# Given SBUF places modulo 256 in every stage, and Newton's root in the first feed-forward of a decoder trunk

## The chip, the core and the metric

The kernel runs on one core of a Trainium2 chip. The metric is the device time of one execution in microseconds (us), as a median of runs. Five engines work side by side: TensorE (PE in the profile; its weight loads are listed apart as PEld), VectorE (DVE), ScalarE (ACT), GpSimd (POOL) and SyncE (SP), which issues most DMAs. Their operands lie in SBUF, 128 partitions wide; TensorE's results land in PSUM.

## The reference

Two layers work on 512 tokens of 1024 features, all in float32. Each layer is a half-step feed-forward, a mixer (a convolution module in layer 0, native sparse attention in layer 1), a second half-step feed-forward, and a gated input embedding; a norm closes the whole.

```python
def rms_norm(x, g):
    xf = x.astype(jnp.float32)
    y = xf * lax.rsqrt(jnp.mean(xf * xf, axis=-1, keepdims=True) + RMS_EPS)
    return (y * g.astype(jnp.float32)).astype(x.dtype)

def swiglu(x, wg, wu, wd):
    return (jax.nn.silu(x @ wg) * (x @ wu)) @ wd
...
    for i in range(DEPTH):
        x = x + 0.5 * swiglu(rms_norm(x, ffn1_norm[i]), ffn1_w_gate[i], ffn1_w_up[i], ffn1_w_down[i])
        h = rms_norm(x, mix_norm[i])
        ...  # conformer_conv for i = 0, nsa_mixer for i = 1
        x = x + 0.5 * swiglu(rms_norm(x, ffn2_norm[i]), ffn2_w_gate[i], ffn2_w_up[i], ffn2_w_down[i])
        gate = jax.nn.sigmoid(rms_norm(x, ple_norm[i]) @ ple_w_gate[i])
        x = x + gate * (p[i] @ ple_w_in[i])
    return rms_norm(x, final_norm)
```

The feed-forward is 1024 -> 2816 -> 1024, twice per layer.

## The kernel before, in words

**Layout.** Activations are held transposed: eight tiles of 128 features x 512 tokens. A matmul has a 128x128 block of a weight as its stationary operand (loaded by LDWEIGHTS) and an activation tile of 512 or 256 tokens as its moving operand.

**Three matmuls for one.** Both operands are split into a high part that the fast float32r format holds exactly and the rest: a weight into `wh` and `wl` (ScalarE copies the high part, line 292; VectorE subtracts, line 294), an activation into two tiles likewise. `mm3` (lines 353 to 358) issues high x high (L356), high weight x low activation (L357), low weight x high activation (L358). Nearly all of TensorE's time in the profile stands under these three lines, so the names of the tiles tell the stages apart: `out<-moving,stationary`.

**Feed-forward.** `ffn` (line 543) goes through 22 tiles of 128 hidden features. The first two are plain: 8 input tiles, 512 columns, moving tiles `s`. The others go in pairs (`pairs`, line 495): a 2x2 block product over two hidden tiles and two halves of 256 tokens with seven products instead of eight, from sums and differences of blocks. Its moving tiles are halves of `s` (the input itself) and `px` (differences of input blocks, made once per feed-forward by `right_sums`, line 475); its stationary tiles are `wh`/`wl` (weights and their combinations, made by `combine`) and `s1hl` (a sum of weights, split, made by `first_sums`, line 320). In one pair, with gate and up taken together, TensorE issues 48 matmuls on `s`, 24 on `px`, 24 on `px` against `s1hl`, 24 on `px`, then twice 12 on `s` and 12 on `px`, all of 256 columns. The gated result is split into `hid` tiles, which are the moving operands of the down projection, 512 columns.

**The norm.** The input is scaled by the gain alone, and the token's factor is multiplied in afterwards. Squares are added up in `acc` (line 432). `token_sums` (line 445) sums `acc` over features by four tiny matmuls against a column of means, `v` adds epsilon (L467), `rsqrt` (line 436) raises it to -0.5 on POOL (L438), and `spread` (L451, L458) turns the result into a tile `R` by four transposes. In the very first feed-forward the input comes straight from DMA, and `acc` is finished while TensorE is already at work on the plain tiles; `SUMS_AT = 3` places the sums in the second plain tile's gate product.

**Order.** The engines run their queues in order. A scheduler at build time orders the instructions from the code's order, priorities (`high_priority`) and explicit ties (`issue_after`): an instruction so tied is placed in the order behind the one it names. Weight splits run a few units ahead of their use (`ahead`, line 334). `behind` ties the splits of pair weights to the last `px` (`righted`).

**Places.** SBUF is given out by pools: constants, weights (`raw`, `wh`, `wl`), slots (`s`, 24 of them), tiny tiles, and a pool per stage (`phase`), whose tags are laid down in the order in which they are first asked for. So where a tile lies, modulo 256 bytes, follows from the sizes ahead of it.

Of the kernel before, what the change touches and what calls it, by code (L numbers as in the profile page):

```python
# [21 lines left out]
TAPS = 31  # L22
X_W1, WARM = 4, 18
OUTS = 2
CONV_FIN = 0
# [10 lines left out]
SUMS_AT = 3  # L36
# [159 lines left out]
class Kern:  # L196
    def __init__(self, ctx, tc, aps):
        self.ctx, self.tc, self.nc = ctx, tc, tc.nc
        self.a = aps
        pool = lambda name, **kw: ctx.enter_context(tc.tile_pool(name=name, **kw))  # L200
        self.cpool = pool("consts", bufs=1)
        self.wpool = pool("weights", bufs=1)
        self.spool = pool("slots", bufs=1)
        self.tiny = pool("tiny", bufs=2)
        self.ppool = pool("ps", bufs=1, space=PSUM)
        self.dpool = pool("dram", bufs=1, space=DRAM)
        self.uid = 0
        self.raw, self.hl, self.sums = {}, {}, {}
        self.unskewed = []
        self.HLB, self.held, self.now = 5, set(), None  # L210
        self.next_raw = self.next_split = 0
# [9 lines left out]

    def ptile(self, tag, n, w=512, dt=F32):
        self.uid += 1
        return self.phase.tile([128, w], dt, name=f"{tag}{self.uid}", tag=tag, bufs=n)
# [44 lines left out]
    def _split(self, what, j):  # L269
# [26 lines left out]
        if pair:  # L296
            with self.behind():
                self.first_sums(j)
# [5 lines left out]
    def combine(self, what, j):  # L304
# [4 lines left out]
        lo, hi = slice(0, HU // 2), slice(HU // 2, HU)  # L309
        q = self.sums[j]  # L310
        if what == "c":
            nc.vector.tensor_tensor(q[:, lo], u[:, lo], t[:, lo], op=OP.subtract)
            nc.vector.tensor_tensor(u[:, lo], t[:, hi], q[:, lo], op=OP.subtract)
# [4 lines left out]
        self.hl[what, j] = (h, l)  # L318

    def first_sums(self, j):  # L320
# [7 lines left out]
        nc.vector.tensor_tensor(u[:, lo], u[:, lo], u[:, hi], op=OP.add)  # L328
        hl = self.ptile("s1hl", 2, HU, F32R)
# [4 lines left out]
    def ahead(self, e):  # L334
# [3 lines left out]
        self.loads()  # L338
        while self.next_split < e:
# [100 lines left out]

    def token_sums(self, p, tiles):
# [19 lines left out]
    def rfin(self, acc):  # L461

        with self.tc.high_priority(FIN_PRI):
# [4 lines left out]
            r = self.rsqrt(v, 4)  # L468
# [74 lines left out]
    def ffn(self, n, i, nxt):  # L543
# [4 lines left out]
        fin = self.rfin(self.acc)  # L548
# [5 lines left out]
        for pi, fs in enumerate(PARTS):  # L554
# [9 lines left out]
            if pi == 0:  # L564
                assert PLAIN == 2
                first = (n, i) == (1, 0)
# [23 lines left out]
                if first:  # L590
                    with self.tc.issue_after(self.squared), self.tc.issue_after(self.vins):
                        for k in range(KD // 2):
                            self.right_sums(f"ffn{n}_norm", i, k)
                else:
# [3 lines left out]
                for f, pg, pu in wait:  # L598
                    gr = self.tmp()
                    nc.vector.tensor_tensor(pg, pg, R, op=OP.mult)  # L600
                    nc.scalar.activation(gr, pg, AF.Silu)
                    gated(f, gr, pu)
            for f in fs[::2]:
# [3 lines left out]
                G = next(both)  # L607
# [104 lines left out]
    def glu(self, c, pa, pg, ta=None):  # L712
# [4 lines left out]
        with self.tc.high_priority(FIN_PRI):  # L717
            nc.vector.tensor_tensor(pg, pg, self.R, op=OP.mult)
            nc.scalar.activation(pg, pg, AF.Sigmoid, bias=self.col("conv_b_pw1", KD + c))
            if CONV_ON[c] == "pe":  # L720
                u = self.ptile("uu", 2, PH * (SP + LAGS - 1)).rearrange("p (q s) -> p q s", q=PH)
# [4 lines left out]
            else:  # L726
                u = self.ptile("u", 3, S + TAPS - 1)
# [103 lines left out]
    def conv(self, nxt):  # L831
# [3 lines left out]
        self.dwc = self.phase.tile([128, KD, TAPS], F32, name="dwc")  # L835
# [159 lines left out]
    def put_k(self, g):  # L995
        nc, t, KT = self.nc, self.kt, self.KTs[g % 2]
        for br, sl, ot in ((0, slice(0, 64), slice(64, 128)), (1, slice(64, 128), slice(0, 64))):
            nc.scalar.activation(KT[sl, 0, br, 32:], t[sl], AF.Copy)
            nc.vector.tensor_tensor(KT[sl, 1, br, 32:], t[sl], KT[sl, 0, br, 32:].bitcast(F32), op=OP.subtract)
            nc.sync.dma_start(KT[ot, :, br, 32:].bitcast(F32), KT[sl, :, br, 32:].bitcast(F32))  # L1000
# [74 lines left out]
    def cmp_in(self, j, first):  # L1075
# [15 lines left out]
        for gp, p in wait:  # L1091
            for s in range(2):
                t = self.ptile("e", EB, 516)
# [54 lines left out]
    def scores(self, job):  # L1148
# [16 lines left out]
        for a in range(HPG):  # L1165
            Q = self.Q[g, a // 2][:, a % 2, qt * 128:qt * 128 + 128]
            src, e = {}, self.slot() if a == HPG - 1 else self.ptile("e", EB, 516)
# [109 lines left out]
    def osplit(self, g):  # L1277
        nc = self.nc
        for pr in range(2):
            t = self.OT[g][pr]  # L1280
            h, l = (self.slot(F32R) if g < 2 else self.ptile("e", EB, 516, F32R)[:, :512] for _ in range(2))
# [26 lines left out]
    def nsa(self, nxt):  # L1308
# [3 lines left out]
        P = self.phase  # L1312
# [3 lines left out]
        self.pos = P.tile([128, 2, 16], F32, name="pos")  # L1316
        nc.gpsimd.dma_start(self.pos, self.a["pos"])
        self.rowmask = P.tile([128, 1], F32, name="rowmask")
        nc.gpsimd.dma_start(self.rowmask, self.a["rowmask"])
        self.gates = P.tile([128, 4, 48], F32, name="gates")  # L1320
        self.gates0 = P.tile([128, 16], F32, name="gates0")
        self.kc = P.tile([128, G, 32], F32, name="kc")
        self.ec = P.tile([128, 4, HPG, 32], F32, name="ec")
# [4 lines left out]
        self.ects = [P.tile([128, 2, 512], F32R, name=f"ect{i}") for i in range(2)]  # L1328
# [111 lines left out]
    def run(self):  # L1440
        def phase():
            return self.tc.tile_pool(name="phase", bufs=1, reuse_waits="tile")
# [3 lines left out]
        for i in range(L):  # L1446
            self.tb = 4
# [84 lines left out]
```

## Time and profile before

| what | value |
|---|---|
| runs | 2019.25 us median of 3 (2018.37 to 2019.88) |
| profiled execution | 2018.77 us, its span 2016.7 us |
| TensorE busy | 1992.7 us, 99% of the span |
| VectorE busy | 1546.0 us, 77% |
| ScalarE / POOL busy | 1100.5 us, 330.7 us |
| matmuls recorded | 12534 |

In a row of a group stand the line of the kernel, the engine, the operation, `out<-in` by the program's names without buffer numbers (`b` is a bank of PSUM), partitions x elements, the count, then the busy time in us and the mean duration of one in ns, and behind the second bar the engine's idle time ahead of these instructions and who ended it. A timeline row begins with the start and the duration in us. A matmul's recorded duration is longer than the distance to the next one's start, since matmuls overlap in the pipeline.

### The profile page before, as it was taken

The numbers are of one execution on the slowest core, as the hardware profiler recorded it, in microseconds if no ns is written. First come the engines' busy times: TensorE is split into PE (matmuls) and PEld (weight loads), VectorE is DVE, ScalarE is ACT, GpSimd is POOL, SyncE is SP. The second block draws the span as 40 slices with busy tenths as digits, with TensorE's granted clock in tenths as the row PEclk, the third lists the DMA queues.
The fourth block names the chain that finished last, engine by engine and source line by source line (L and its number), as shares of the span: only waits on it lengthen the run. The fifth ranks groups of instructions, "written<-read, shape, count | busy, mean of one in ns | idle before, by whom it ended". The sixth has DMA issues, their size and how long they took to land.

```text
span 2016.7 us, 32709 instructions
## 1 busy us (share of the span) xinstructions
PE 1992.7 (99%) x12534; PEld 1789.7 (89%) x12534; DVE 1546.0 (77%) x2703; ACT 1100.5 (55%) x1972; POOL 330.7 (16%) x365
## 2 busy tenths in 40 slices
PE   8999999999999999999999999999999999999998
PEld 7989999888789898988999989888888789998987
DVE  8869777795687796777968868646889797786875
ACT  7535445662665363555644535437888665363543
POOL 0000000352300000012000000557666200000022
PEclk9999999999999999999999999999999999999999
DMA  4323323466425244243232322463333023232241
GB/s 170 105 96 104 126 74 105 180 206 202 141 97 166 86 144 136 97 133 118 84 115 95 115 87 90 162 182 116 95 90 104 25 99 120 95 116 94 94 141 59
DMA packets 79483, 235.16 MB, mean 117 GB/s; under 512 B 8848, under 2 KB 16160, under 8 KB 79328
## 3 DMA queue, kind: packets, MB, share of 16 engines
q1 hardware_dynamic: 78368, 230.69, 34.6%
q8 instruction: 98, 1.61, 0.3%
q0 software_dynamic: 816, 2.33, 0.3%
q14 instruction: 57, 0.47, 0.1%
q10 hardware_dynamic: 144, 0.07, 0.0%
HBM read 214.66 MB, written 16.29 MB: 115 GB/s over the span
## 4 chain that ended last, share of the span: by engine, by line
PE 91%; DVE 6%; ACT 2%; issue 1%; DMA 0%; SPq 0%; POOL 0%; DVEq 0%; POOLq 0%; ACTq 0%
PE b L356 28%; PE b L357 27%; PE b L358 27%; PE b L821 2%; PE b L1180 1%; PE b L1244 1%; PE b L1263 1%; PE b L1119 1%; PE b L1264 1%; DVE s L415 1%; DVE t L482 1%; DVE wl L294 1%; DVE px L491 0%; DVE acc L432 0%; DMA raw<-in_w 0%
## 5 line engine op out<-in xcount | busy, mean ns | idle before, releaser
L356 PE MATMUL b<-s,wh 128*128 128x256 f32 (+1 forms) x1408 | 448.8, 320 | 0.6 <-ACT wh L292 0.5
L357 PE MATMUL b<-s,wh 128*128 128x256 f32 (+1 forms) x1408 | 447.5, 318 | 0.9 <-DVE s L415 0.6
L358 PE MATMUL b<-s,wl 128*128 128x256 f32 (+1 forms) x1408 | 446.3, 319 | 0.2 <-DVE wl L294 0.2
L292 ACT ACTIVATE wh<-raw 128x1024 fp32r<-128x1024 f32 (+1 forms) x251 | 263.7, 1054 | 256.5 <-PE b L357 174.1
L357 PE MATMUL b<-px,wh 128*128 128x256 f32 (+1 forms) x1112 | 321.5, 289 | 1.7 <-DVE px L491 1.7
L356 PE MATMUL b<-px,wh 128*128 128x256 f32 (+1 forms) x1112 | 321.4, 290 | 0.7 <-ACT G L503 0.7
L358 PE MATMUL b<-px,wl 128*128 128x256 f32 (+1 forms) x1112 | 321.5, 289 | 0.0
L294 DVE TENSOR_TENSOR wl<-raw,wh 128x1024 fp32r<-128x1024 f32 (+1 forms) x205 | 251.0, 1226 | 68.9 <-ACT wh L292 68.4
L356 PEld LDWEIGHTS b<-s,wh 128*128 128x128 f32 x1408 | 268.3, 191 | 19.2 <-ACT wh L292 1.1
L357 PEld LDWEIGHTS b<-s,wh 128*128 128x128 f32 x1408 | 268.0, 190 | 19.5 <-DVE s L415 1.9
L358 PEld LDWEIGHTS b<-s,wl 128*128 128x128 f32 x1408 | 267.5, 191 | 17.7 <-DVE wl L294 0.5
L358 PE MATMUL b<-hid,wl 128*128 128x512 f32 x704 | 275.3, 393 | 0.0
L357 PE MATMUL b<-hid,wh 128*128 128x512 f32 x704 | 274.5, 391 | 0.0
L356 PE MATMUL b<-hid,wh 128*128 128x512 f32 x704 | 269.7, 390 | 0.0
L294 POOL TENSOR_TENSOR wl<-raw,wh 128x1024 fp32r<-128x1024 f32 (+1 forms) x53 | 128.5, 2431 | 709.8 <-ACT wh L292 709.6
L503 ACT ACTIVATE G<-b 128x256 f32<-128x256 f32 x400 | 145.1, 377 | 141.7 <-PE b L358 122.6
L357 PEld LDWEIGHTS b<-px,wh 128*128 128x128 f32 x1112 | 209.5, 188 | 7.0 <-DVE px L491 2.1
L356 PEld LDWEIGHTS b<-px,wh 128*128 128x128 f32 x1112 | 209.5, 189 | 6.0 <-ACT G L503 1.3
L358 PEld LDWEIGHTS b<-px,wl 128*128 128x128 f32 x1112 | 209.4, 188 | 3.8
L357 PEld LDWEIGHTS b<-hid,wh 128*128 128x128 f32 x704 | 132.2, 188 | 29.4
L356 PEld LDWEIGHTS b<-hid,wh 128*128 128x128 f32 x704 | 132.2, 188 | 28.1
L358 PEld LDWEIGHTS b<-hid,wl 128*128 128x128 f32 x704 | 132.1, 188 | 27.5
(246 smaller groups left out, 3624.4 us busy)
## 6 DMA issues: line engine op xcount, KB each, us to landing
raw<-in_w SPq DMA_DIRECT2D x255, 512.0 KB, 3.3
rawx<-in_w SPq DMA_DIRECT2D x80, 512.0 KB, 3.3
tw<-in_tw SPq DMA_DIRECT2D x20, 576.0 KB, 6.8
skew<-table SPq DMA_DIRECT2D x16, 320.0 KB, 5.8
z<-t SPq DMA_DIRECT2D x16, 256.0 KB, 2.2
hid<-z SPq DMA_DIRECT2D x16, 256.0 KB, 4.1
tt<-skew SPq DMA_DIRECT2D x16, 256.0 KB, 3.0
wr<-in_w SPq DMA_DIRECT2D x8, 512.0 KB, 4.1
```

Source lines behind the costliest of these rows:

```text
L292: nc.scalar.activation(h[:, c], t[:, c], AF.Copy)
L294: eng.tensor_tensor(l[:, c], t[:, c], h[:, c].bitcast(F32), op=OP.subtract)
L356: mm(out, sh, mh, start=start, stop=False, **how)
L357: mm(out, sh, ml, start=False, stop=False, **how)
L358: self.lastmm = mm(out, sl, mh, start=False, stop=stop, **how).ins
L415: b = nc.vector.scalar_tensor_tensor(view(l), x, g, view(h.bitcast(F32)), op0=OP.mult, op1=OP.subtract)
L482: sub = lambda o, x, y: nc.vector.tensor_tensor(o, x, y, op=OP.subtract)
L503: copy = lambda o, x: nc.scalar.activation(o, x, AF.Copy)
L821: nc.tensor.matmul(p[:, q * SP:q * SP + SP], T[q][:, d * 128:d * 128 + 128], u[:, q, o:o + SP], start=d == 0, stop=d == LAGS - 1)
L1119: nc.tensor.matmul(P[mh][:, :124], w, B[kk // 4][:, kk % 4, :], start=kk == 0, stop=kk == 15)
L1180: nc.tensor.matmul(p[:, :32 - lo + nk], Q, KT[:, i, "sw".index(b), lo:32 + nk], start=i == 0, stop=i == 1)
L1244: nc.tensor.transpose(p[:, a * 128:a * 128 + 128], J[a, b][:, kt * 128:kt * 128 + 128], self.ident)
```

## The change

**Places.** Two pads (`gap0` of 64 bytes ahead of the slots, `gap1` of 128 ahead of the stage pools) and a bookkeeping of each stage's pool: `place` counts the bytes laid down so far in the stage (`top`) and puts a pad ahead of a tag whose place modulo 256 is prescribed. `AT` prescribes it for seven tags; `own` does the same for tiles that stand alone, of which `vc`, the `v` tiles and `ect` are put at 0 and `kt` at 128. The tiles `e`, `u`, `uu` and the parts of `kt` become 576 elements wide (516 to 544 before), that is 9 times 256 bytes, so that all buffers of a tag lie at one place. In the built programs the tiles lie, modulo 256 bytes:

| tile | before | after |
|---|---|---|
| `wh`, `wl`, `raw` | 192 | 192 |
| `s` | 192 | 0 |
| `s1hl` | 0 | 192 |
| `px` | 0 | 0 |
| `hid` | 0 | 192 |
| `tw` | 224 | 192 |
| `zp` | 96 | 192 |
| `e` | 0 to 224, spread | 192 |
| `kt` | 224 (its data at 96 and 224) | 128 (its data at 0) |
| `q`, `t` (attention, feed-forward), `G` | 0 | 0 |
| `v`, `vc`, `ect` | 224 | 0 |

For the main moving/stationary pairs, that is: 256 columns, `s`/`wh` from 192/192 to 0/192, `px`/`s1hl` from 0/0 to 0/192, `px`/`wh` 0/192 as before; 512 columns, `hid`/`wh` from 0/192 to 192/192, `s`/`wh` from 192/192 to 0/192.

**The first feed-forward of layer 0.** `rfin(steps=True)` takes the root on VectorE: `root_steps`, a bit-trick start and three Newton steps, ten instructions of 128x4. The token sums are tied behind seven of the eight inputs' matmuls of the first plain tile, and the next step of the norm (the transposes) behind the second plain tile's gate product. The `px` work (`right_sums`) is tied behind the root instead of behind `v`; the column sums of the first pair's weights (`sum_parts`, split off `first_sums`) and one of the differences of `combine` are put off until behind the last `px` (`lazy`); `cap` keeps the weight splits from running ahead of that; the gates of the plain tiles are put off behind `righted` too. The stage has 6 `t` tiles instead of 4.

```diff
+PAD_SLOTS, PAD_PHASE = 16, 32
+AT = {"s1hl": 192, "G": 0, "px": 0, "hid": 192, "tw": 192, "e": 192, "tt": 0}
+UW = 576
...
-SUMS_AT = 3
+NEWTON = 3
...
+        pool("gap0", bufs=1).tile([128, PAD_SLOTS], F32, name="gap0")
         self.spool = pool("slots", bufs=1)
         self.tiny = pool("tiny", bufs=2)
+        pool("gap1", bufs=1).tile([128, PAD_PHASE], F32, name="gap1")
...
+    def place(self, tag, size, at=None):
+        pad = 0 if at is None else (at - self.top) % 256
+        if pad:
+            self.uid += 1
+            self.phase.tile([128, pad // 4], F32, name=f"gap{tag}{self.uid}", tag=f"gap{tag}", bufs=1)
+        self.top += pad + -(-size // 32) * 32
...
     def ptile(self, tag, n, w=512, dt=F32):
+        if tag not in self.tags:
+            self.tags.add(tag)
+            self.place(tag, n * (-(-w * 4 // 32) * 32), AT.get(tag))
...
         if pair:
-            with self.behind():
-                self.first_sums(j)
+            if j not in self.lazy:
+                with self.behind():
+                    self.first_sums(j)
+                    self.sum_parts(j)
...
+    def root_steps(self, v, n):
+
+        nc = self.nc
+        y = self.tiny.tile([128, 4], F32, name="r", tag="r")[:, :n]
+        a = self.tiny.tile([128, 4], F32, name="ra", tag="ra")[:, :n]
+        nc.vector.tensor_scalar(y.bitcast(I32), v.bitcast(I32), -0.5, float(0x5f3759df), op0=OP.mult, op1=OP.add)
+        for _ in range(NEWTON):
+            nc.vector.tensor_tensor(a, y, y, op=OP.mult)
+            nc.vector.scalar_tensor_tensor(a, a, -0.5, v, op0=OP.mult, op1=OP.mult)
+            self.root = nc.vector.scalar_tensor_tensor(y, a, 1.5, y, op0=OP.add, op1=OP.mult).ins
+        return y
...
                         for ks in (range(KD - 1), (KD - 1,)):
                             plain(pg, g, f, ks)
                             plain(pu, u, f, ks)
+                            if first and len(ks) > 1:
+                                with self.tc.issue_after(self.lastmm):
+                                    next(fin)
                     for p, nm in ((pg, g), (pu, u)) if f else ():
-                        if first and p is pg:
-                            plain(p, nm, f, range(SUMS_AT))
-                            with self.tc.issue_after(self.lastmm):
-                                next(fin)
-                            plain(p, nm, f, range(SUMS_AT, KD))
-                        else:
-                            plain(p, nm, f)
+                        plain(p, nm, f)
...
-                    with self.tc.issue_after(self.squared), self.tc.issue_after(self.vins):
-                        for k in range(KD // 2):
+                    for k in range(KD // 2):
+                        with self.tc.issue_after(self.squared), self.tc.issue_after(self.root if k else self.summed):
                             self.right_sums(f"ffn{n}_norm", i, k)
...
-        self.vc = P.tile([128, G, 128], F32R, name="vc")
-        self.KTs = [P.tile([128, 2, 2, 544], F32R, name=f"kt{i}") for i in range(2)]
-        self.Vs = [P.tile([128, 8, 128], F32R, name=f"v{i}") for i in range(2)]
+        self.vc = self.own("vc", [128, G, 128], F32R, at=0)
+        self.KTs = [self.own(f"kt{i}", [128, 2, 2, UW], F32R, at=128) for i in range(2)]
+        self.Vs = [self.own(f"v{i}", [128, 8, 128], F32R, at=0) for i in range(2)]
...
-            self.tb = 4
+            self.tb = 6 if i == 0 else 4
```

How this moves instructions in the first feed-forward, on TensorE first. Before, behind the third plain product (72 matmuls on `s`), the four sums (`meanr,acc`) and the four transposes (`ident,r`) stand together:

```order
L358 MATMUL b_282<-s_179,wl_139 128x512
L445 MATMUL b_301<-meanr,acc_183 128x1 x4
L451 MATMUL b_325<-ident,r 128x128 x4
L356 MATMUL b_283<-s_151,wh_144 128x512
L357 MATMUL b_283<-s_152,wh_144 128x512
```

With the change, the sums stand behind 48 matmuls:

```order
L398 MATMUL b_215<-s_188,wh_140 128x512
L399 MATMUL b_215<-s_187,wl_141 128x512
L498 MATMUL b_264<-meanr,acc_191 128x1 x4
L397 MATMUL b_289<-s_159,wh_146 128x512
L398 MATMUL b_289<-s_160,wh_146 128x512
L399 MATMUL b_289<-s_159,wl_147 128x512
```

and the transposes 24 matmuls further on:

```order
L398 MATMUL b_289<-s_188,wh_146 128x512
L399 MATMUL b_289<-s_187,wl_147 128x512
L504 MATMUL b_315<-ident,r 128x128 x4
L397 MATMUL b_290<-s_159,wh_152 128x512
L398 MATMUL b_290<-s_160,wh_152 128x512
```

So the sums are 24 matmuls earlier, and between sums and transposes there is now a whole product.

On VectorE, behind the last sum of squares (`acc`), before: the first pair's weight sums (L327, L328, L312, L331) and two splits, then `v`:

```order
L432 TENSOR_TENSOR acc_183<-acc_183,t_203 128x512
L327 TENSOR_TENSOR sq_218<-raw_142,rawx_208 128x512
L328 TENSOR_TENSOR rawx_208<-rawx_208 128x512
L312 TENSOR_TENSOR sq_218<-rawx_208,raw_142 128x512
L294 TENSOR_TENSOR wl_145<-raw_136,wh_144 128x1024
L294 TENSOR_TENSOR wl_215<-raw_142,wh_214 128x1024
L331 TENSOR_TENSOR s1hl_221<-rawx_208,s1hl_221 128x512
L467 TENSOR_SCALAR v<-b_301 128x4
L482 TENSOR_TENSOR t_363<-G_362 128x512
```

With the change, three steps of the first `px`, then `v` and the root's ten, with a split and two `px` among them:

```order
L473 TENSOR_TENSOR acc_191<-acc_191,t_211 128x512
L535 TENSOR_TENSOR t_347<-G_346 128x512
L535 TENSOR_TENSOR t_348<-G_346,t_347 128x256
L535 TENSOR_TENSOR t_348<-G_346,t_348 128x256
L520 TENSOR_SCALAR v<-b_264 128x4
L487 TENSOR_SCALAR r<-v 128x4
L489 TENSOR_TENSOR ra<-r 128x4
L490 SCALAR_TENSOR_TENSOR ra<-ra,v 128x4
L317 TENSOR_TENSOR wl_153<-raw_144,wh_152 128x1024
L491 SCALAR_TENSOR_TENSOR r<-ra,r 128x4
L489 TENSOR_TENSOR ra<-r 128x4
L544 TENSOR_TENSOR px_354<-t_347,px_354 128x512
```

The weight sums that stood ahead of `v` now stand behind the root, and `s1hl` behind all eight `px`. On SP nothing moves; on POOL the root's one instruction and the load of its library go from the head of the program. Elsewhere the order of the engines stays, but for a few rows at the end of the attention stage.

More of the change, by code (lines that the diff above doesn't have):

```diff
@@ L209, in __init__ @@
         self.unskewed = []
-        self.HLB, self.held, self.now = 5, set(), None
+        self.HLB, self.held, self.now, self.cap = 5, set(), None, None
+        self.lazy = ()
         self.next_raw = self.next_split = 0
@@ L220, in tmp, with own @@
         return self.ptile("t", self.tb, dt=dt)
+    def place(self, tag, size, at=None):
[4 more added lines that the diff above has]
+        self.top += pad + -(-size // 32) * 32
+    def own(self, name, shape, dt=F32, at=None):
+        size = 4
+        for n in shape[1:]:
+            size *= n
+        self.place(name, size, at)
+        return self.phase.tile(shape, dt, name=name)
     def ptile(self, tag, n, w=512, dt=F32):
+        if tag not in self.tags:
+            self.tags.add(tag)
+            self.place(tag, n * (-(-w * 4 // 32) * 32), AT.get(tag))
         self.uid += 1
@@ L309, in combine @@
         lo, hi = slice(0, HU // 2), slice(HU // 2, HU)
+        lazy = what == "c" and j in self.lazy
+        if lazy:
+            self.first_sums(j)
         q = self.sums[j]
@@ L318, in combine @@
         self.hl[what, j] = (h, l)
+        if lazy:
+            with self.tc.issue_after(self.righted):
+                self.sum_parts(j)
+                nc.vector.tensor_tensor(u[:, lo], t[:, hi], q[:, lo], op=OP.subtract)
     def first_sums(self, j):
@@ L338, in ahead @@
         self.loads()
+        if self.cap is not None:
+            e = min(e, self.cap)
         while self.next_split < e:
@@ L459, in spread, with rfin @@
         return R
-    def rfin(self, acc):
+    def rfin(self, acc, steps=False):
         with self.tc.high_priority(FIN_PRI):
@@ L547, in ffn @@
         self.now, self.T4 = (f"ffn{n}", i), []
-        fin = self.rfin(self.acc)
+        first = (n, i) == (1, 0)
+        if first:
+            self.lazy = [PLACE[nm, i, 0, PLAIN][0] for nm in (g, u)]
+            self.cap = ENTRY["s", self.lazy[0]]
+        fin = self.rfin(self.acc, steps=first)
         def plain(p, nm, f, ks=range(KD)):
@@ L597, in ffn, with plain_gates @@
                 R = self.R
[L598 to L602, printed above, removed]
+                def plain_gates():
+                    for f, pg, pu in wait:
+                        gr = self.tmp()
+                        nc.vector.tensor_tensor(pg, pg, R, op=OP.mult)
+                        nc.scalar.activation(gr, pg, AF.Silu)
+                        gated(f, gr, pu)
+                if not first:
+                    plain_gates()
             for f in fs[::2]:
@@ L606, in ffn @@
                 both = self.pairs((g, u), i, f)
-                G = next(both)
+                with self.tc.issue_after(self.root) if first and f == PLAIN else nullcontext():
+                    G = next(both)
+                if first and f == PLAIN:
+                    with self.tc.issue_after(self.righted):
+                        plain_gates()
                 nc.vector.tensor_tensor(G, G, R[:, None, :].to_broadcast([128, 2, 512]), op=OP.mult)
@@ L834, in conv @@
         X, U, Y = self.X, {}, []
-        self.dwc = self.phase.tile([128, KD, TAPS], F32, name="dwc")
+        self.dwc = self.own("dwc", [128, KD, TAPS])
         nc.gpsimd.dma_start(self.dwc, self.a["dwc"])
@@ L1280, in osplit @@
             t = self.OT[g][pr]
-            h, l = (self.slot(F32R) if g < 2 else self.ptile("e", EB, 516, F32R)[:, :512] for _ in range(2))
+            h, l = (self.slot(F32R) if g < 2 else self.ptile("e", EB, UW, F32R)[:, :512] for _ in range(2))
             nc.scalar.activation(h, t, AF.Copy)
@@ L1441, in phase @@
         def phase():
+            self.tags, self.top = set(), 0
             return self.tc.tile_pool(name="phase", bufs=1, reuse_waits="tile")
```

44 lines of the change are left out of this document (26 added, 18 removed).

## The prediction

> **What bounds the kernel now.** I read the head of the page first, then the chain of work that ended last, then the groups of instructions with their shapes kept apart, then the timeline of TensorE at single stages.
>
> ```profile
> span 2016.7 us, 32709 instructions
> PE 1992.7 (99%) x12534; PEld 1789.7 (89%) x12534; DVE 1546.0 (77%) x2703; ACT 1100.5 (55%) x1972; POOL 330.7 (16%) x365
> PE 91%; DVE 6%; ACT 2%; issue 1%; DMA 0%; SPq 0%; POOL 0%; DVEq 0%; POOLq 0%; ACTq 0%
> ```
>
> TensorE is busy 99% of the span and holds 91% of the chain. So what counts is how far apart the starts of its matmuls lie, and the few places where it stands still. VectorE is busy 77% of the span and sets 6% of the chain, DMA none of it, so both can feed a TensorE that is a per cent faster.
>
> ```profile
> L356 PE MATMUL b<-px,wh 128*128 128x256 f32 x1008 | 281.0, 280 | 0.7 <-ACT G L503 0.7
> L358 PE MATMUL b<-px,wl 128*128 128x256 f32 x1008 | 280.3, 278 | 0.0
> L356 PE MATMUL b<-s,wh 128*128 128x256 f32 x960 | 271.3, 283 | 0.3 <-ACT wh L292 0.3
> L357 PE MATMUL b<-px,s1hl 128*128 128x256 f32 x320 | 90.1, 283 | 0.2 <-DVE px L491 0.2
> L356 PE MATMUL b<-hid,wh 128*128 128x512 f32 x704 | 269.7, 390 | 0.0
> L358 PE MATMUL b<-hid,wl 128*128 128x512 f32 x704 | 275.3, 393 | 0.0
> L357 PE MATMUL b<-s,wh 128*128 128x512 f32 x448 | 176.4, 394 | 0.9 <-DVE s L415 0.6 <-DVE s L1283 0.2
> L356 PE MATMUL b<-px,wh 128*128 128x512 f32 x104 | 40.4, 389 | 0.0
> L358 PE MATMUL b<-px,wl 128*128 128x512 f32 x104 | 41.1, 396 | 0.0
> L357 PE MATMUL b<-tw,wh 128*128 128x512 f32 x64 | 25.1, 395 | 0.0
> L357 PE MATMUL b<-zp,wh 128*128 128x512 f32 x32 | 12.7, 396 | 0.0
> L358 PE MATMUL b<-e,wl 128*128 128x512 f32 x32 | 12.6, 395 | 0.0
> ```
>
> The same 128x256 matmul lasts 283 ns with `s` against `wh` and with `px` against `s1hl`, but 278 to 280 with `px` against the weights. In the table of places, the first two have both operands at one place modulo 256 (192/192 and 0/0), the third has them apart (0/192). The recorded duration holds a pipelined tail, so the timeline gives the price: one pair of f tiles, and then two 512-column stretches.
>
> ```profile
> 268.02 0.28 PE L356 MATMUL b<-s,wh 128*128 128x256 f32 x1
> ...
> 273.78 0.28 PE L356 MATMUL b<-px,wh 128*128 128x256 f32 x1
> ...
> 276.61 0.28 PE L356 MATMUL b<-px,s1hl 128*128 128x256 f32 x1
> ...
> 279.48 0.28 PE L356 MATMUL b<-px,wh 128*128 128x256 f32 x1
> ...
> 282.20 0.28 PE L356 MATMUL b<-s,wh 128*128 128x256 f32 x1
> ```
>
> From 268.02 there are 48 matmuls on `s`: 5.76/48 = 120.0 ns from start to start. Then 24 each of `px` against `wh`/`wl` (2.83/24 = 117.9), `px` against `s1hl` (2.87/24 = 119.6), and `px` against `wh`/`wl` again (2.72/24 = 113.3). So the apart-lying pair has two spells, slow (117.9) behind the `s` run and fast (113.3) behind the `s1hl` run, and each keeps its step to the end of its run. The pair then closes with two times 12 on `s` and 12 on `px`, the latter behind `s`, so slow: of 72 such matmuls a pair has 24 fast ones, a mean of 116.4.
>
> ```profile
> 261.84 0.39 PE L356 MATMUL b<-hid,wh 128*128 128x512 f32 x1
> ...
> 267.79 0.39 PE L358 MATMUL b<-hid,wl 128*128 128x512 f32 x1
> ...
> 964.25 0.39 PE L357 MATMUL b<-s,wh 128*128 128x512 f32 x1
> ...
> 969.24 0.39 PE L358 MATMUL b<-s,wl 128*128 128x512 f32 x1
> ```
>
> At 512 columns it is the other way round. `hid` against the weights (0/192, apart) makes 26 steps in 5.95 us, 228.8 ns; `s` against the weights (192/192, equal) makes 22 in 4.99, 226.8.
>
> **The change part by part.** *256 columns.* The change puts `s` at 0 and `s1hl` at 192, so all three kinds lie at 0/192. There are 3 x 960 = 2880 matmuls on `s`, 3 x 320 = 960 on `s1hl`, and 3 x 1008 = 3024 on `px` against weights. The unknown is which spell each run falls into. Bounds from the same rows: all slow, 3840 x (120.0 - 117.9) = 8.1 gained on the first two, and 3024 x (117.9 - 116.4) = 4.5 lost on `px`, whose fast third needed the `s1hl` run at 0/0 ahead of it; net -3.6. All fast: 3840 x 6.7 = 25.7 and 3024 x 3.1 = 9.4; net -35.1. A third fast, as today on `px`: 3840 x 3.6 = -13.8. Half fast (115.6): -16.9 - 2.4 = -19.3. I take -16.5, between the last two: the spell is set at the entry into a run, by what stood ahead of it, and both come today; no row shows an entry behind a `hid` at 192, so I lean on neither end.
>
> *512 columns.* `hid` goes to 192, equal: 2112 x (228.8 - 226.8) = -4.2. `s` goes to 0, apart: 1344 x 2.0 = +2.7. Its bound above is the state of the `px` row of line 358 at 396 ns, against 389 at line 356: 1344 x 6.6 = +8.9; below, 0, since the mean of `s` today, 394, is no better than that of `px`. `tw`, `zp` and `e` (395 or so, about 64 + 32 + 32 times three matmuls) are put at equal places; they fall to the 389 or 390 of the equal stretch: 384 x 5.5 = -2.1. The two products of `t` with `v` and the scores of `kt` with `q` also become equal, 224 matmuls; no quoted row gives their step, and with the same 5.5 it is -1.2. Sum of these: -4.2 + 2.7 - 3.3 = -4.8, bounds -7.5 to +4.
>
> The Trainium skill speaks against all of this: "TensorE: Matmul & The Clock Gate", section "Step-by-step: what each phase is for", gives TensorE two independent SBUF read ports, one for the moving operand and one for the weights, so that where the two lie should not matter. The trace disagrees: same shape, same stationary width, 113.3 to 120.0 ns. By the page alone the address part would be worth 0; that is a rival below.
>
> *First feed-forward.* Here the root leaves POOL and the token sums come 24 matmuls earlier.
>
> ```profile
> 19.29 2.28 DVE L432 TENSOR_TENSOR acc<-acc,t 128x512 f32<-128x512 f32 x3
> ...
> 20.55 0.39 PE L357 MATMUL b<-s,wh 128*128 128x512 f32 x1
> ...
> 25.76 0.95 PE L445 MATMUL b<-meanr,acc 128*128 128x1 f32 x8
> ...
> 27.63 0.15 DVE L467 TENSOR_SCALAR v<-b 128x4 f32<-128x4 f32 x1
> ...
> 27.87 1.41 POOL L438 TENSOR_TENSOR r<-v,power 128x4 f32<-128x4 f32 x1 [25.86 <-DVE v L467]
> ...
> 29.33 0.65 PE L451 MATMUL b<-ident,r 128*128 128x128 f32 x4 [2.62 <-POOL r L438]
> ...
> 30.77 0.63 PE L357 MATMUL b<-s,wh 128*128 128x512 f32 x1
> ...
> 34.16 0.39 PE L356 MATMUL b<-s,wh 128*128 128x512 f32 x1
> ```
>
> Today TensorE waits 2.62 us: the sums end at 26.71, `v` waits in VectorE's queue until 27.63, POOL takes 1.41 us. From 30.77 to 34.16 it then runs 8 matmuls at 424 ns, half clock: 3.39 - 8 x 0.227 = 1.6 us more. Both go, since after the change 24 matmuls (5.4 us) stand between sums and transposes, and VectorE needs less: `v` and ten small steps at 0.15 us or less are 1.7 us, with one 1024-element split and two 512-element steps between them, some 2.4 us. Removed: 4.2. What is late next is the accumulator: the 48 matmuls ahead of the sums are issued by 20.55, the last `acc` step ends at 21.57, and TensorE now waits that 1.0 us, with every later matmul queued behind it. That wait and the 0.95 us of one-column sums lie within one stretch of 3.4 us, and may bring a half-clock stretch of their own, another 1.6. So -3.2 or -1.6.
>
> Behind the root stands VectorE's backlog:
>
> ```profile
> 20.00:40.00 20.00, 17.38 (x89) 14.84 (x88) 18.62 (x30) 13.43 (x22) 1.41 (x1) 0.91 0.24 80
> 40.00:60.00 20.00, 18.73 (x139) 18.03 (x137) 20.00 (x33) 13.60 (x23) 0.00 (x0) 0.91 0.23 80
> 50.02 0.38 PE L357 MATMUL b<-px,wh 128*128 128x256 f32 x1 [0.83 <-DVE px L491]
> 50.99 0.43 PE L356 MATMUL b<-px,wh 128*128 128x256 f32 x1 [0.24 <-ACT G L503]
> 51.23 0.41 PE L357 MATMUL b<-px,wh 128*128 128x256 f32 x1
> ```
>
> In these windows (TensorE, weight loads, VectorE, ScalarE, POOL, then TensorE's clock) VectorE is full for 20 of 20 us from 40 on, and TensorE waits for `px` and then runs at half clock (0.41 instead of 0.28). The change gives VectorE 1.5 us of small steps and a wait for the sums; it also sorts `px` ahead of the column sums of the weights (`s1hl`), so the wait at 50.02 may move to `s1hl`. Bounds: 2.7 won if the stall and its half clock go, 2.7 lost if they double. With nothing on this and the mean of the two cases above, -2.5; bounds -6 to +1. POOL is all but idle there, so its place in the root was no burden elsewhere. The root library's load moves to the convolution's root, hidden behind work that has POOL idle for hundreds of us.
>
> On the clock the trace comes first: two half-speed stretches follow stalls, of 2.62 us and of 0.83 + 0.24. The Trainium skill, same page, section "What's actually happening", says that the clock gate looks at a free-running window of about 3.4 us. The stretch from 30.77 to 34.16, 3.39 us, agrees in length. By that rule the new 1.0 us wait alone is less than a window and would not halve the clock, and the term were -3.2; but the 1.07 us ahead of 51.23 did.
>
> *Rest.* SP's order is unchanged. At the end of the attention stage a few instructions change places near a stall that the trace has there; I cost it at 0, with 2 us to either side. The wider `e`, `u`, `uu` and `kt` tiles cost SBUF, not time: their instructions are the same size.
>
> Sum against the profiled execution (2016.7 in the span and 2.07 around it, 2018.77): -16.5 - 4.8 - 2.5 = -23.8, 1995.0. The median 2019.25 is 0.5 above that execution; I forecast 1995.
>
> **Rivals.** *All slow*: entries into 0/192 behind `s` and `hid` are slow, and the fast third goes: -3.6 - 4.8 - 2.5 = -10.9, 2008. For it: 273.78 to 276.61, slow behind a run whose moving tile lay at 192, where `hid` now lies. Against: that run was at 256 columns.
> *All fast*: the moving tile stays at 0 throughout, as it did from `s1hl` into the fast spell at 279.48: -35.1 - 4.8 - 2.5 = -42.4, 1976.5.
> *The addresses do nothing*, since the 283 and 280 ns belong to the tiles' roles (what writes them, which product they serve): only the first feed-forward is left, -2.5, 2016.5. Against: `px` has both numbers, in runs next to each other.
> *Slower*: 0/192 has a slower spell, and long unbroken runs fall into it. At 512 columns the rows show it, 396 against 389. Carried to 256 columns, 117.9 x 396/389 = 120.0 for all 6864 matmuls: 3024 x 3.6 = +10.9 and 0 on the rest; `s` at 512 columns in the same state +8.9, `hid`, `tw` and the others -7.5, the first feed-forward -2.5: +9.8, 2029. It decides from where the 256-column mean passes about 119.2 (today's is (3840 x 120.0 + 3024 x 116.4)/6864 = 118.4, and the rest comes to -1.1). For it: nothing at 256 columns.
>
> **How the numbers follow.** The mixed case, the forecast, 0.47 (own range 1989 to 2000); all slow 0.27; all fast 0.15; addresses nothing 0.07; slower 0.04. About 0.2%, 4 us, is what a measurement of this kernel can tell from no change. Faster is the first three, 0.89; within 0.2% is the fourth, 0.07; slower 0.04. The range goes from 1977, which takes in half of the fast case, to 2009, the slow case with a little of its unknown tail; left out are half of the fast case, the fourth and the fifth, 0.19.
>
> **What would show it.** In the groups, `s` and `px,s1hl` at 128x256 fall from 283 to 276 to 281, and `px,wh` shows the spell; 276 everywhere is the fast case, 281 the slow one. `hid` goes to 389 or 390 in all three lines, `s` at 512 columns rises to 391 to 396, `tw` and `e` fall under 391. The wait for POOL's `r` at the first transposes is gone, one for `acc` of about 1 us stands at the sums, and the rows near 30 us run at full clock. The prediction is wrong if `s` stays at 283, if `s` or `px` at 256 columns passes 282, or if the first feed-forward shows more idle time than the 2.62 + 1.27 us that 20 to 60 us has now.

## The result

The changed kernel takes 2007.48 us (median of 6 runs, 2007.14 to 2008.83) against 2018.88 us before, a ratio of 0.9944 with a 95% interval of 0.9932 to 0.9957: 11.4 us faster. The forecast was 1995, the range 1977 to 2009; the time is that of the rival called all slow, 2008. In direction the forecast held; the gain it gave, 24 us, was twice the measured one.

The head of the page of the changed kernel, and then its groups with their shapes apart (lines 397 to 399 are the three matmuls of `mm3`, 356 to 358 before):

```profile
span 2005.4 us, 32696 instructions
PE 1980.8 (99%) x12534; PEld 1782.9 (89%) x12534; DVE 1546.8 (77%) x2713; ACT 1098.9 (55%) x1972; POOL 329.9 (16%) x364
```

```profile
L397 PE MATMUL b<-px,wh 128*128 128x256 f32 x1008 | 281.5, 280 | 1.3 <-ACT G L556 1.3
L398 PE MATMUL b<-hid,wh 128*128 128x512 f32 x704 | 273.1, 389 | 0.0
L399 PE MATMUL b<-hid,wl 128*128 128x512 f32 x704 | 272.9, 389 | 0.0
L397 PE MATMUL b<-s,wh 128*128 128x256 f32 x960 | 267.9, 280 | 0.8 <-ACT wh L315 0.5 <-ACT G L556 0.3
L398 PE MATMUL b<-s,wh 128*128 128x512 f32 x448 | 175.7, 392 | 1.4 <-DVE s L456 1.2 <-DVE s L1350 0.2
L398 PE MATMUL b<-px,s1hl 128*128 128x256 f32 x320 | 89.0, 279 | 0.0
L398 PE MATMUL b<-tw,wh 128*128 128x512 f32 x64 | 24.7, 389 | 0.0
```

TensorE lost 11.9 us of busy time, the other engines 2 us or less. `s` and `px` against `s1hl` fell from 283 to about 280 ns, `hid` to 389 in all lines, `tw` from 395 to 389. But `px` against the weights did not go on falling: 280, as before or a little more. One pair of f tiles in the timeline, at the places where the kind of matmul changes, says why:

```profile
263.27 0.28 PE L397 MATMUL b<-s,wh 128*128 128x256 f32 x1
...
268.93 0.28 PE L397 MATMUL b<-px,wh 128*128 128x256 f32 x1
...
271.75 0.28 PE L397 MATMUL b<-px,s1hl 128*128 128x256 f32 x1
...
274.58 0.28 PE L397 MATMUL b<-px,wh 128*128 128x256 f32 x1
...
277.41 0.28 PE L397 MATMUL b<-s,wh 128*128 128x256 f32 x1
```

48 matmuls in 5.66 us, then three times 24 in 2.82, 2.83 and 2.83: 117.9, 117.5, 117.9, 117.9 ns. Everything of 256 columns goes in the slow spell, also the run at 274.58 that stepped at 113.3 before the change. Of all 6857 steps within 256 columns in this trace, 226 lie in a fast spell; none of them is in the second or third part of a feed-forward. (A feed-forward's ten pairs come in parts of 3, 4 and 3, each followed by its share of the down projection.)

In the first feed-forward, the page's timeline shows the sums and the transposes, and the windows (columns as in the prediction) show the clock:

```profile
22.02 1.05 PE L498 MATMUL b<-meanr,acc 128*128 128x1 f32 x8 [1.11 <-DVE acc L473]
...
28.53 0.60 PE L504 MATMUL b<-ident,r 128*128 128x128 f32 x4
...
47.22 0.38 PE L397 MATMUL b<-px,wh 128*128 128x256 f32 x1 [0.83 <-ACT G L556]
```

```profile
20.00:40.00 20.00, 18.89 (x112) 16.34 (x112) 19.48 (x41) 14.76 (x23) 0.00 (x0) 1.00 0.16 54
40.00:60.00 20.00, 18.79 (x154) 18.11 (x153) 19.77 (x31) 12.39 (x23) 0.00 (x0) 1.00 0.32 106
```

No wait for the root is left, the wait for `acc` is 1.11 us, and the clock is 1.00 in both windows, 0.91 before. The waits behind the root did not go, they moved: 0.83 and 0.32 us for `G`, and 0.64 for a `wl` at 66 us, where before 1.0 us for `px` and 0.24 for `G` stood. From 20 to 75 us TensorE waits 3.1 us in all, 3.9 before.

### The profile page after: what moved, and what is told of

Same layout as the page of the kernel before. It is cut to its first block, busy times and chain, and to the rows that moved or that the text cites. A ratio compares the mean times of both kernels' runs of the same rounds, so it can differ in the third digit from the quotient of the medians.

```text
span 2005.4 us, 32696 instructions
## 1 busy us (share of the span) xinstructions
PE 1980.8 (99%) x12534; PEld 1782.9 (89%) x12534; DVE 1546.8 (77%) x2713; ACT 1098.9 (55%) x1972; POOL 329.9 (16%) x364
## 4 chain that ended last, share of the span: by engine, by line
PE 90%; DVE 6%; ACT 2%; DMA 1%; issue 1%; SPq 0%; POOL 0%; DVEq 0%; ACTq 0%; POOLq 0%
PE b L397 27%; PE b L398 27%; PE b L399 27%; PE b L888 2%; PE b L1247 1%; PE b L1311 1%; DMA raw<-in_w 1%; PE b L1330 1%; PE b L1331 1%; PE b L1186 1%; DVE t L535 1%; DVE wl L317 0%; DVE s L456 0%; DVE px L544 0%; DVE acc L473 0%
## 5 line engine op out<-in xcount | busy, mean ns | idle before, releaser
L397 PEld LDWEIGHTS b<-s,wh 128*128 128x128 f32 x1408 | 264.5, 188 | 20.4 <-ACT wh L315 2.2
L398 PEld LDWEIGHTS b<-s,wh 128*128 128x128 f32 x1408 | 264.0, 188 | 20.2 <-DVE s L456 2.4
```

The source lines that it names most:

```text
L397: mm(out, sh, mh, start=start, stop=False, **how)
L398: mm(out, sh, ml, start=False, stop=False, **how)
```

## The experiments

Steps from start to start that no row gives are taken from the same traces, matmul by matmul, with the tiles' places from the built programs; steps with a wait in them and those at half clock (213 ns and more at 256 columns) are left out of the means. Fast means 115 ns or less, slow 117 to 119.

**The two parts apart.** One kernel has the changed places with the old first feed-forward, the other the old places with the new first feed-forward (`PAD_PHASE` and one pad are set so that the extra tiny tile `ra` doesn't shift the places).

```diff
 e1: after.py with _split, combine, first_sums, ahead, rfin, ffn as in before.py
-PAD_SLOTS, PAD_PHASE = 16, 32
+PAD_SLOTS, PAD_PHASE = 16, 48
-            self.tb = 6 if i == 0 else 4
+            self.tb = 4
 e2: before.py with the same methods, sum_parts and root_steps as in after.py
+        pool("gap1", bufs=1).tile([128, 48], F32, name="gap1")
```

> The changed places, with the first feed-forward as in the kernel before. Read from the two traces, the changed kernel gained 3.9 us by the end of the first gate and up products of layer 0 and 8.2 us from there to the end. If the two parts add up, this run is some 8 us faster than before, about 2011, its first transposes wait 2.6 us for POOL again, and at 256 columns all three kinds are at 279 to 280 ns. The rival, that the faster first feed-forward only brings forward waits which the places then uncover, has this run at 2007 to 2008, as fast as the whole change.

> The changed first feed-forward, with all tiles at the places of the kernel before. If the parts add up: 3.5 to 4 us faster than before, about 2015, no wait for the root, a wait of 1.1 us for acc at the sums, and 283 ns for s and for px against s1hl at 256 columns. The rival, that the places carry nothing and the whole gain is this part's, has it at 2007 to 2008.

Measured: places alone 2011.39, ratio 0.9963 (0.9951 to 0.9976); first feed-forward alone 2015.47, ratio 0.9984 (0.9975 to 0.9993). They add up: -7.1 and -3.0 us make -10.1, and the whole change had -11.4. The timeline of the first kernel keeps the wait for POOL at the transposes; that of the second has the wait for `acc` at the sums, and below it stands its window from 20 to 40 us:

```profile
29.91 0.65 PE L497 MATMUL b<-ident,r 128*128 128x128 f32 x4 [2.58 <-POOL r L472]
```

```profile
22.43 1.05 PE L477 MATMUL b<-meanr,acc 128*128 128x1 f32 x8 [1.18 <-DVE acc L452]
```

```profile
20.00:40.00 20.00, 18.82 (x96) 15.84 (x95) 19.48 (x41) 15.28 (x24) 0.00 (x0) 0.91 0.17 54
```

So the places do matter, and the rivals in which either part does all fall. In the second kernel the 1.18 us wait is followed by a half-clock stretch (0.91 in its window), in the changed kernel the 1.11 us wait is not (1.00): the half-clock stretch that the prediction left open can come and can stay away. The kernel `e3` below, whose first feed-forward differs from the changed one's by the place of `s1hl` alone, has a 1.12 us wait there and the half-clock stretch with it (0.91). So the place of the wait in the program does not settle it. That much agrees with the rule of the Trainium skill that the prediction named ("TensorE: Matmul & The Clock Gate", "What's actually happening"), a window that runs freely, though none of these runs shows where the windows begin; that page also asks for a whole idle window of about 3.4 us, and here 1.18 us of waiting, with 1.05 us of one-column sums behind it, was enough.

**Is the root on VectorE needed?** The changed kernel with POOL's root:

```diff
-PAD_SLOTS, PAD_PHASE = 16, 32
+PAD_SLOTS, PAD_PHASE = 16, 48
...
-        fin = self.rfin(self.acc, steps=first)
+        fin = self.rfin(self.acc)
```

> The changed kernel with the root of the first feed-forward left to POOL as before; the token sums stay early. By my step the sums end 5.5 us ahead of the transposes and POOL needs 1.4 us and the way there and back 1.7 in all, so TensorE does not wait for the root either way, and the gain is that of the early sums: the same time as the changed kernel within 1 us, 2007.5. The rival, that the root on VectorE is needed: the wait returns in part or px comes later, 2009 to 2010.

Measured 2008.06 (2006.54 to 2009.67), ratio to before 0.9948 (0.9935 to 0.996): that of the changed kernel within the interval. The timeline of the sums, POOL's root and the transposes:

```profile
23.28 1.05 PE L498 MATMUL b<-meanr,acc 128*128 128x1 f32 x8 [0.39 <-DVE acc L473]
26.77 1.14 POOL L479 TENSOR_TENSOR r<-v,power 128x4 f32<-128x4 f32 x1 [24.77 <-DVE v L520]
29.79 0.60 PE L504 MATMUL b<-ident,r 128*128 128x128 f32 x4
```

POOL is done at 27.91, the transposes start at 29.79 without a wait. So it does not matter here who takes the root. What pays is in the rest of the new order; the early sums are the likeliest part, since the wait at the transposes goes with them, but the runs do not part them from the later weight sums, `px` and gates.

**Is the spell a matter of history?** Three kernels move `s1hl` alone. First, back to 0 in the changed kernel:

```diff
-AT = {"s1hl": 192, "G": 0, "px": 0, "hid": 192, "tw": 192, "e": 192, "tt": 0}
+AT = {"s1hl": 0, "G": 0, "px": 0, "hid": 192, "tw": 192, "e": 192, "tt": 0}
```

> The changed kernel with s1hl alone put back to 0. Theory of history: whether a pair at 0/192 steps at 113.3 or 117.8 ns is settled at the entry into the stretch and stays until a matmul of another kind (512 columns, or both operands at one place) comes in between; a run at 0/0 leaves the fast one behind. Then s1hl itself goes back to 119.6 (960 matmuls, +1.7 us), and all that stands behind it in a pair, 72 matmuls, and in the next pair the 72 ahead of s1hl, where the pairs stand next to each other (about 28 of 40), run at 113.3: about 4900 x 4.5 = -22, so about 1987, with 276 ns for most of px and s at 256 columns. Rival one, that only the run straight behind s1hl is fast (as in the kernel before): 960 x 4.5 - 1.7, about 2005. Rival two, that the fast spell needs s at 192: +1.7, about 2009.

Measured 1992.26 (1991.5 to 1993.15), ratio to before 0.987 (0.9856 to 0.9883). Putting one tile back to a place where its own matmuls are slower makes the kernel 15 us faster. Its groups, and in its timeline the end of one part of a feed-forward:

```profile
L397 PE MATMUL b<-px,wh 128*128 128x256 f32 x1008 | 278.9, 277 | 0.5 <-ACT G L556 0.5
L398 PE MATMUL b<-s,wh 128*128 128x256 f32 x960 | 265.0, 277 | 0.0
L398 PE MATMUL b<-px,s1hl 128*128 128x256 f32 x320 | 90.2, 283 | 0.0
```

```profile
208.29 0.28 PE L399 MATMUL b<-px,s1hl 128*128 128x256 f32 x1
...
209.85 0.28 PE L397 MATMUL b<-px,wh 128*128 128x256 f32 x1
...
212.57 0.28 PE L397 MATMUL b<-s,wh 128*128 128x256 f32 x1
...
218.01 0.39 PE L397 MATMUL b<-hid,wh 128*128 128x512 f32 x1
```

`px` against `s1hl` is back at 283, and the 72 matmuls behind it, `px` and `s` alike, take 8.16 us, 113.3 ns each. Of the 5864 steps on `s` and on `px` against the weights 4187 are fast and 1654 slow; in the changed kernel 225 of 5861 are fast. The 1654 stand mostly at the heads of the second and third parts, in front of the first run at 0/0 (72 each time), and in the first parts. This is less than the 4900 expected and gives 15 us, not 20; but neither rival (2005, 2009) is near.

Second, `s1hl` moved to 192 in the kernel before, and nothing else:

```diff
+            if tag == "s1hl":
+                self.phase.tile([128, 48], F32, name=f"gapa{self.uid}", tag="gapa", bufs=1)
+                ...  # s1hl itself, then 64 bytes, so that all behind it stays in place
```

> The kernel before with s1hl alone put to 192. Theory of history: px against the weights, whose own places do not change, loses the fast run behind s1hl: 960 x 4.6 = +4.4 us, and s1hl gains 960 x 1.8 = 1.7, so 2.7 slower, about 2021.5; px against wh at 256 columns goes from 276 to 280 behind s1hl, and its mean from 279 to 280 or 281. The rival, that the step depends on the places of the running pair alone: 1.7 faster, about 2017, and px as before.

Measured 2021.14, ratio 1.0013 (1.0004 to 1.0022): 2.6 us slower, as expected, although the moved tile's own matmuls went from 283 to 279 ns. `px` against the weights, untouched, lost most of its fast steps (1163 of 2979 before, 257 of 2988 here; mean 116.2 before, 117.6 here). Its group of `s1hl`, and the pair whose rows the prediction shows, from the `s1hl` run on:

```profile
L366 PE MATMUL b<-px,s1hl 128*128 128x256 f32 x320 | 89.0, 279 | 0.2 <-DVE px L500 0.2
```

```profile
275.97 0.28 PE L365 MATMUL b<-px,s1hl 128*128 128x256 f32 x1
...
278.79 0.28 PE L365 MATMUL b<-px,wh 128*128 128x256 f32 x1
...
281.62 0.29 PE L365 MATMUL b<-s,wh 128*128 128x256 f32 x1
```

The 24 `px` behind `s1hl` take 2.83 us, 117.9 ns each; in the kernel before they took 2.72 us, 113.3.

Third, only the gate's `s1hl` at 0 and that of up at 192 (two tags with one buffer each instead of one with two):

```diff
-        hl = self.ptile("s1hl", 2, HU, F32R)
+        self.sides = 1 - self.sides
+        hl = self.ptile(("s1hl", "s1hm")[self.sides], 1, HU, F32R)
```

> e3 with s1hl of the gate left at 0 and that of up put to 192. By the theory of history the 12 matmuls of the gate at 0/0 are enough to leave the fast spell behind, and the 12 of up then step at 113.3 instead of 119.9: 480 x 6.6 = 3.2 us faster than e3, about 1989. If the 12 that come last decide (up at 0/192 behind a fast stretch does not hold it), px behind them goes slow: about 2004.

Measured 1990.74 (1990.37 to 1991.16), ratio 0.9864 (0.9847 to 0.988): 1.5 us faster than the kernel with both at 0, half of what was expected, and the intervals of the two ratios overlap. Its groups of the two tiles:

```profile
L401 PE MATMUL b<-px,s1hl 128*128 128x256 f32 x160 | 45.2, 283 | 0.0
L401 PE MATMUL b<-px,s1hm 128*128 128x256 f32 x160 | 44.3, 277 | 0.0
```

`s1hm`, up's tile, is at 277 now, which is worth 2.6 us. But shorter runs at 0/0 do not always suffice. The last pair of each second part is slow for 84 matmuls: there the scheduler puts eleven of the gate's twelve ahead of 12 `px`, which are fast, and a single one at 0/0 right ahead of the 84. At two places even a full run of twelve leaves the slow spell behind it, and some slow stretches go on through a whole further pair. So 3606 steps on `s` and `px` are fast, against 4187, which costs the 2.6 us again: in the two traces the four feed-forwards, from their first pair to their last `hid`, take 1258.6 us with both at 0 and 1258.9 here. The 1.5 us stand elsewhere, in the attention stage (341.4 and 339.4 us), where this edit changes nothing; why it is shorter was not looked into. The expectation came half true in the time, but not for its reason. This is the fastest kernel of the study, 28 us faster than before and 17 faster than the change.

**The 512-column term, and a surprise.** `hid` alone back to 0 in the changed kernel:

```diff
-"hid": 192
+"hid": 0
```

> The changed kernel with hid alone put back to 0. From the steps of the two traces (228.2 and 230.5 ns against wh and wl before, 227.0 and 226.9 after): 1400 x 1.2 + 700 x 3.6 = 4.2 us slower than the changed kernel, about 2011.5. If equal places do nothing at 512 columns and the difference is one of spells, 2007.5.

Measured 2006.89, but the six runs lie between 2000.03 and 2010.94, where the changed kernel's six lie within 1.7 us. The profiled run is the fastest of them. Its timeline, at the first and the last matmul of the second part of a feed-forward (4 pairs, 672 matmuls of 256 columns), in layer 0's first and layer 0's second:

```profile
141.52 0.28 PE L397 MATMUL b<-s,wh 128*128 128x256 f32 x1
...
217.68 0.39 PE L397 MATMUL b<-hid,wh 128*128 128x512 f32 x1
...
680.72 0.28 PE L397 MATMUL b<-s,wh 128*128 128x256 f32 x1
...
759.86 0.39 PE L397 MATMUL b<-hid,wh 128*128 128x512 f32 x1
```

76.16 us and 79.14 us for the same work: 113.3 and 117.8 ns a step, over 672 matmuls without a change. So the spell is set at the entry behind the down projection and then holds, and with `hid` at 0/192, whose steps wander between 226 and 232 ns, it differs from one part to the next: of the eight second and third parts four are fast, those of the first and of the last feed-forward. That it differs between executions as well is inferred from the times, since only one was traced: the four fast parts are worth (2 x 672 + 2 x 504) x 4.5 ns = 10.6 us, and 10.9 lie between the fastest and the slowest run. Behind `hid` at 192/192, with its even 227, all eight of these parts are slow in the trace of the changed kernel, and 16 of its 19 entries behind `hid`. The size of the term for `hid` itself was right: in this trace it steps at 229.0 and 228.8 against `wh` and `wl`, 227.0 and 226.9 in the changed kernel, 4.1 us over 2093 steps; the median hides it behind the fast parts.

**A map of the places.** The kernel with `s1hl` at 0, the five buffers of `wh` and of `wl` spread over five places:

```diff
+WAT = (224, 64, 96, 128, 160)   # places of the five buffers; each has a tag of its own
```

> A map of the step by place: e3 (s and px at 0, hid at 192, s1hl at 0) with the five buffers of wh and of wl at 224, 64, 96, 128 and 160 modulo 256 instead of all at 192. Nothing else moves; the weights change place every unit, so the total time is not the point. If only equality modulo 256 counts, all five places step like 192 against 0, at 113 to 118 ns for 256 columns and 227 to 234 for 512. If the step follows the distance modulo 128, weights at 128 step at 120 with s and px, as at 0, and weights at 64 like those at 192. If the distance matters finely, the five differ from each other and one of them may be faster or slower than all that was seen, down to 110 or up to 125.

A single run, 2039.77. Mean steps and the commonest ones, in ns, by the distance of the stationary tile from the moving one modulo 256; steps where the distance had just changed are left out:

```
distance   256 columns, s or px      512 columns, s or hid
32         not seen                  233.3
0          119.8 (120)               227.0 (226, 227), changed kernel
64         114.6 to 114.9 (113, 114, 117, 118)   233.3
96         118.5 to 119.2 (120)      234.4
128        119.1 to 119.3 (115 to 123)   232.6 to 233.2
160        119.9 (116, 121, 125)     233.3 to 233.4
192        113.3 or 117.8 (e3)       228.8 (226, 229, 232)
224        116.7 to 116.9 (113, 116, 120)   233.4 to 233.8
```

The distance matters finely, and the two widths want different things: 0 is best at 512 columns, 64 and 192 at 256, each with the same two spells. Neither a rule modulo 128 nor one of equal or not holds. The runs at one distance are short here, so these are not all settled states.

**Moving the run at 0/0 to the head of the pair.** If the spell is set there, it should stand first.

```diff
+        if early:
+            for n in range(2):
+                product(n, side[n][:, hi], "e", 0, T1, True)
+                copy(G[n][:, 1, 0], side[n][:, hi])
 e7:  early = f != PLAIN
 e10: early = pi > 0 and f == fs[0], and start = not early on the product of B21
```

In e7 the start flag of the B21 product, now the second in its bank, discards the product of `px` and `s1hl`; the work on the engines is the same, the product is missing from the result.

> e3 with the products of px against s1hl put at the head of every pair but the first of a feed-forward, instead of in its middle. In e3 the trace still has some 76 matmuls of 256 columns at 117.8 ns ahead of the first run at 0/0 of each part that follows a down projection. By the theory of history the run at 0/0 now comes first there, so 8 to 11 parts gain 76 x 4.5 = 0.34 us each, 3 to 4 us: about 1988.5, and hardly any slow stretch is left behind a down projection. If the spell is not kept from the run at 0/0 on, or s1hl comes too late from VectorE, 1992 or more.

> e3 with the products of px against s1hl at the head of the pair only where the pair follows a down projection (8 pairs in all), and with the bank's start flag on the product that comes first. By the theory of history these 8 pairs lose their 76 slow matmuls: 8 x 76 x 4.5 = 2.7 us, about 1989.5; the rows behind the down projections show 113 ns from the run at 0/0 on. If s1hl comes late from VectorE there, the wait eats it: 1992 or more.

> e10 with s1hl of the gate at 0 and that of up at 192, as in e6. e6 was 1.5 us faster than e3, so about 1988 if the two add up. If 12 matmuls at 0/0 are too few to leave the fast spell behind a down projection, as they were at several places of e6, no gain over e10.

Measured 2008.01, 1998.79 and 1998.27 (ratios 0.9946, 0.9906, 0.9903): all slower than e3's 1992.26. The spells did much as expected: in e10 the 72 slow matmuls that e3 has at the heads of the second and third parts are fast. Some others turn slow, since the last matmuls of a part now stand behind its first `hid` (12 in a second part, 60 in a third). On balance there are 4621 fast steps against 4187, worth 2.0 us, and the four feed-forwards are 1.8 us shorter than in e3. The loss is elsewhere. In e7 new waits stand in the list of TensorE's waits (in all, times, longest), one of the two largest of them first below. In e10 6.1 us are lost at the head of the attention stage, within 40 matmuls behind the down projection: its timeline and its window from 1270 to 1290 us follow, and then the same window of e3.

```profile
PE b L397 <- ACT s1hl L369: 3.6, 1, 3.6
```

```profile
1281.69 0.79 PE L397 MATMUL b<-s,wh 128*128 128x512 f32 x1 [1.95 <-ACT s L455]
```

```profile
1270.00:1290.00 20.00, 16.53 (x64) 12.60 (x63) 14.64 (x17) 7.28 (x11) 11.73 (x14) 0.83 0.48 172
```

```profile
1270.00:1290.00 20.00, 19.76 (x92) 15.61 (x91) 10.51 (x15) 7.11 (x10) 15.32 (x16) 1.00 0.57 185
```

TensorE waits for `s` there and its clock falls to 0.83 in the window, 1.00 in e3. What the scheduler does differently at that place when eight pairs change their order was not followed up, so this version stays a promise, not a result.

## Why the prediction was wrong

**256 columns: the step that failed.** The prediction bounded this term between -3.6 (all slow) and -35.1 (all fast) and took -16.5, because "the spell is set at the entry into a run, by what stood ahead of it, and both come today ... so I lean on neither end". By the steps in the two traces it was -4.4: `s` 120.0 to 117.8 (-6.3), `s1hl` 119.7 to 117.8 (-1.9), `px` against the weights 116.2 to 117.5 (+3.8). The first half of the quoted sentence is what e3, e4 and e9 show. The second did not follow from it. If the spell is set by what stands ahead, one has to ask which entries are left after the change, and the change takes away the only one that the prediction had seen lead into the fast spell, the run at 0/0. The prediction wrote this down as the first rival, with its price of 4.5 us on `px`, and then averaged over spells as if each run had its own draw. With the run at 0/0 gone, a part keeps the spell of its entry behind the down projection, and the prediction said itself that no row showed this entry. So all slow deserved more than its 0.27, but that it would be all slow no row could tell; e9 shows that with `hid` left at 0 half of the long parts can be fast. The number of that rival, 2008, was right within a microsecond, and its three terms, -3.6, -4.8 and -2.5, each within 1 us of what is measured here.

**512 columns: right.** Predicted -4.2 for `hid`, +2.7 for `s`, -3.3 for the rest, -4.8 in all. The traces give -4.3, +1.9 and about -2.5, some -4.8 in all; `t` against `v` gained next to nothing. The upper bound of this term does not come out of its own figures: -4.2 + 8.9 - 3.3 is +1.4, not +4. The sum does not rest on it.

**First feed-forward: right in size, partly in cause.** Predicted -2.5, measured -3.0 by e2 (its interval goes from -1.4 to -5.0). The wait for `acc` was predicted as 1.0 us and is 1.11. The second half-clock stretch, at 51 us, is gone in the changed kernel, which the prediction had only as a bound. The waits behind the root did not double; they went from `px` to `G` and `wl`, 1.8 us together against 1.3. That Newton's root is needed was never a step of the sum; e8 shows that it isn't.

**The rest.** The three terms as measured come to -12.2 us, against -11.4 in the time; the 0.8 us between them are less than the 1.7 us over which the six runs lie. That the addresses do nothing, which the Trainium skill's two read ports ("TensorE: Matmul & The Clock Gate", "Step-by-step: what each phase is for") would have meant, falls with e1 and, far more clearly, with e3 and e4, where one tile's place moves the time by 15 and 2.6 us. The slower rival needed a third spell above 119.2 ns at 0/192; none appeared.

What stays open is why the place of two operands moves the step at all, why one distance has two stable steps, and what at the entry picks one. The runs show that a run at 0/0 leaves the fast spell behind it in most cases (55 of 63 in the kernel before, 55 of 69 in e3), that a stretch keeps its spell until the kind of matmul changes or TensorE stands still, and that the spell behind a down projection can differ between parts of one execution; they do not show a mechanism. Nor is a run at 0/0 the only way in: near the end, 120 `px` behind 512-column ones step at 113.3 in the kernel before and in the changed one alike.

## What to carry to other kernels

Where two steps of the same work differ in one trace and each is steady, look for what precedes them, and then ask which of these predecessors the change leaves in place; a mean over states is no forecast of a state. Change one place at a time: the tile that sets the pace can be one that is itself slower. And where runs of one kernel spread more than those of its neighbours, look for a state that may differ from execution to execution before comparing medians.

## What the runs showed that was not expected

The same 672 matmuls, with the same shapes and the same places modulo 256, stand in one trace at 113.3 and at 117.8 ns from start to start (76.16 and 79.14 us). With the down projection's matmuls even (227 ns instead of 226 to 232), the entries behind them are nearly all slow, so a gain of 4.1 us on one kind of matmul can cost a like sum on the next. And a 512-column and a 256-column matmul want different places: at distance 0 the one is at the best that was seen, 227, and the other at 120, 6.5 ns above the best seen at its width.
